# Moving a SwiGLU kernel's stores from GpSimd's queue to ACT's, with the critical section closed without a drain of GpSimd

## The chip, the cores and the metric

The program uses one core of one Trainium2 chip. The metric is device time in microseconds (us), the median of several executions. All executions that are compared here are in the fast state, at a granted clock of 1.0; only e6_hold18, a single look that differs by 14%, has an unknown state. The kernel before takes 938.4 us.

## The reference

```python
def setup_inputs():
    return {"x": np.random.randn(8192, 8192).astype(np.float32)}

def reference(x):
    a, b = np.split(x, 2, axis=-1)
    return a * (b / (1 + np.exp(-b)))        # (8192, 4096)
```

256 MiB are read once and 128 MiB are written once, 402.65 MB in all.

## The kernel before

Two rows of x lie on each partition, so a tile is 128 partitions x 16384 floats (8 MiB), and there are 32 tiles. Three slots hold them in turn. SyncE loads, ACT makes silu of the b half in place, DVE multiplies and packs the product into the front of the same slot, and a store of 4 MiB takes it away. Every engine counts semaphores by hand, inside a critical section in which nothing is ordered automatically. The last tile is cut up so that its last store is small.

```python
def load(i, c0=0, cw=R * M):
    s = i % BUFS
    if i >= BUFS:                                     # the slot must have been stored
        nc.sync.wait_ge(store_sem[s], 16 * (i // BUFS))
    nc.sync.dma_start(out=slots[s][...], in_=xv[...]).then_inc(last_sem if c0 else load_sem[s], 16)

def store(i, eng, c0=0, cw=R * half):
    eng.wait_ge(prod_sem, counts["prod"])             # all products issued so far
    inst = eng.dma_start(out=ov[...], in_=slots[s][:, c0 : c0 + cw])
    # ... completion on store_sem[s], for the last tiles on end_sem

with tc.tile_critical():
    # ... three loads
    for i in range(last):
        swiglu(i)                                     # ACT, then DVE (tile 0 in two halves)
        if i == last - 1:
            swiglu(last, 0, 1)                        # first half of the last tile
        store(i, nc.gpsimd if i < last - 1 else nc.sync)
        # ... load of tile i + 3
    # ... the rest of the last tile; SyncE waits for every store
```

## Time and profile before

| | before |
|---|---|
| median of the first 3 executions | 938.40 us (938.26 to 939.66) |
| profiled span | 936.7 us |
| bytes moved | 402.66 MB, 430 GB/s over the span |
| DMA engines, share of the span | 68.4% loads and the last stores, 31.1% GpSimd's stores |
| DVE / ACT / GpSimd busy | 30% / 24% / 2% |
| last store landed | 933.0 us |
| drain of GpSimd at the end | 2.506 us |

### The profile page before, as it was taken

The numbers are of one execution on the slowest core, as the hardware profiler recorded it, in microseconds if no ns is written. First come the engines' busy times: TensorE is split into PE (matmuls) and PEld (weight loads), VectorE is DVE, ScalarE is ACT, GpSimd is POOL, SyncE is SP. The second block draws the span as 40 slices with busy tenths as digits, with TensorE's granted clock in tenths as the row PEclk, the third lists the DMA queues.
The fourth block names the chain that finished last, engine by engine and source line by source line (L and its number), as shares of the span: only waits on it lengthen the run. The fifth ranks groups of instructions, "written<-read, shape, count | busy, mean of one in ns | idle before, by whom it ended". The sixth has DMA issues, their size and how long they took to land.

```text
span 936.7 us, 196 instructions
## 1 busy us (share of the span) xinstructions
DVE 278.6 (30%) x35; ACT 226.6 (24%) x36; POOL 16.3 (2%) x34
## 2 busy tenths in 40 slices
DVE  0333312333123331233312333213332133331351
ACT  0323331133311333113332033320233302333131
POOL 0000000000000000000000000000000000000000
DMA  9999999999999999999999999999999999999997
GB/s 403 403 448 425 425 448 425 427 441 453 406 465 406 451 423 428 446 424 448 424 448 417 453 413 452 418 439 434 442 425 428 445 424 432 434 453 413 434 435 336
DMA packets 9504, 402.66 MB, mean 430 GB/s; under 512 B 1056, under 2 KB 1056, under 8 KB 1056
## 3 DMA queue, kind: packets, MB, share of 16 engines
q1 hardware_dynamic: 5184, 276.83, 68.4%
q0 software_dynamic: 4320, 125.83, 31.1%
HBM read 268.44 MB, written 134.22 MB: 430 GB/s over the span
## 4 chain that ended last, share of the span: by engine, by line
DMA 80%; DVE 10%; ACT 8%; issue 0%; SPq 0%; DVEq 0%
DMA out_dram<-slot 40%; DMA slot<-in_x_dram 40%; DVE slot L72 10%; ACT slot L67 8%; SPq L48 0%; SPq L138 0%; DVEq L71 0%; SPq L89 0%
## 5 line engine op out<-in xcount | busy, mean ns | idle before, releaser
L72 DVE TENSOR_TENSOR slot<-slot 128x8192 f32<-128x8192 f32 (+2 forms) x35 | 278.6, 7960 | 641.6 <-ACT slot L67 641.5
L67 ACT ACTIVATE slot<-slot 128x8192 f32<-128x8192 f32 (+2 forms) x35 | 225.3, 6443 | 689.8 <-DMA slot<-in_x_dram 689.8
L80 POOL DMA_DIRECT2D out_dram<-slot x30 | 16.1, 536 | 857.8 <-DVE slot L72 857.8
L67 ACT ACT_TABLE_LOAD x1 | 1.3, 1283 | 0.9 <-SPq L89 0.9
L127 POOL MEMSET const-float32-0.0<- 128x1 f32 x1 | 0.1, 98 | 0.2 <-issue 0.2
L127 POOL MEMSET const-bfloat16-1.0<- 128x1 bf16 x1 | 0.1, 101 | 0.0
L127 POOL MEMSET const-float32-1.0<- 128x1 f32 x1 | 0.1, 98 | 0.0
L127 POOL MEMSET const-uint8-127<- 128x1 uint8 x1 | 0.1, 98 | 0.0
## 6 DMA issues: line engine op xcount, KB each, us to landing
out_dram<-slot POOLq DMA_DIRECT2D x30, 4096.0 KB, 37.4
slot<-in_x_dram SPq DMA_DIRECT2D x2, 4096.0 KB, 26.4
out_dram<-slot SPq DMA_DIRECT2D x1, 4096.0 KB, 11.3
out_dram<-slot SPq DMA_DIRECT2D x2, 2048.0 KB, 14.2
slot<-in_x_dram SPq DMA_DIRECT2D x31, 33.6
```

The lines of the kernel that those rows point to most:

```text
L67: nc.scalar.activation(out=b, in_=b, func=_SILU).then_inc(gate_sem, 1)
L72: nc.vector.tensor_mul(out=rows(xt, k0, k1, half, c0, cw), in0=rows(xt, k0, k1, M, c0, cw), in1=b).then_inc(prod_sem, 1)
L80: inst = eng.dma_start(out=ov[i * P : (i + 1) * P, c0 : c0 + cw], in_=slots[s][:, c0 : c0 + cw])
L127: nc = _bacc.Bacc("TRN2", target_bir_lowering=False, num_devices=1)
```

## The change

Its intent: stores off GpSimd's software queue and onto ACT's hardware queue, so that the closing drain of GpSimd can be left out; and one explicit wait less at the end, because the store of tile 29 now counts on the semaphore that the end waits for anyway.

```diff
-        if i < last - 1:
+        if i + BUFS <= last:
             inst.then_inc(store_sem[s], 16)
         else:
             inst.then_inc(end_sem, 16)
             counts["end"] += 1
 
-    with tc.tile_critical():
+    with tc.tile_critical(no_gpsimd_drain=True):
...
-            store(i, nc.gpsimd if i < last - 1 else nc.sync)
+            store(i, nc.scalar if i < last - 1 else nc.sync)
...
-        nc.sync.wait_ge(store_sem[(last - 2) % BUFS], 16 * ((last - 2) // BUFS + 1))
         nc.sync.wait_ge(end_sem, 16 * counts["end"])
```

## The prediction

> **What bounds the kernel now.** I read the page's slices first, then its queues, then the DMA share of chosen windows, then the chain of waits, and last the end of the program, instruction by instruction. The slices and the queues:
>
> ```profile
> DMA  9999999999999999999999999999999999999997
> ...
> q1 hardware_dynamic: 5184, 276.83, 68.4%
> q0 software_dynamic: 4320, 125.83, 31.1%
> HBM read 268.44 MB, written 134.22 MB: 430 GB/s over the span
> ```
>
> The sixteen DMA engines are full in every slice but the last. The two queues together take 68.4 + 31.1 = 99.5% of the span of 936.7 us, so only about 0.5% of it, 4.7 us, has no packet in flight. The remaining 932 us are bytes. Windows cut from the trace (us, busy time of DVE, ACT and POOL, PEclk, DMA share, GB/s) place those 4.7 us:
>
> ```profile
> 0.00:1.50 1.50, 0.00 (x0) 0.59 (x1) 0.20 (x4) 1.00 0.00 0
> ...
> 584.00:671.00 87.00, 26.07 (x3) 21.09 (x3) 1.53 (x4) 1.00 1.00 434
> ...
> 920.00:930.00 10.00, 0.22 (x1) 0.00 (x0) 0.00 (x0) 1.00 1.01 433
> ...
> 933.00:936.70 3.70, 0.00 (x0) 0.00 (x0) 0.00 (x0) 1.00 0.00 0
> ```
>
> About 1 us lies before the first load and 3.7 us after the last store. In the middle, 87 us move three tiles at 434 GB/s with a share of 1.00. The compute engines are far from it: DVE is busy 26 of 87 us.
>
> The chain of waits (start, us, what) walks one slot round and round:
>
> ```profile
> 583.42 0.28 issue
> 583.70 37.41 DMA out_dram<-slot
> 621.11 0.02 issue
> 621.13 33.57 DMA slot<-in_x_dram
> 654.70 0.02 issue
> 654.72 7.04 ACT slot L67
> 661.76 0.02 issue
> 661.78 8.70 DVE slot L72
> ```
>
> One turn of a slot is 37.41 + 33.57 + 7.04 + 8.70 + 0.34 = 87.06 us, and three slots make 29.0 us for each tile. This chain looks like latency, but it isn't: one store carries 4 MiB, which at 434 GB/s takes 9.7 us alone, and one load of 8 MiB takes 19.3 us alone. 9.7 + 19.3 = 29.0 us, exactly the period. The 37 and 34 us are times shared with the other slots' transfers. So shortening one link of this chain lengthens another, as long as the DMA engines have no hole.
>
> The lines that the change does touch at the end are those of the critical section's closing (engine, instruction, count, duration in ns min/median/max, start in us):
>
> ```profile
> L89 SPq NOP  x2: 13/13/13, 0.7 to 935.8; - x2
> ...
> L89 ACTq DRAIN  x1: 8/8/8, 933.3 to 933.3; - x1
> L89 POOLq DRAIN  x1: 2506/2506/2506, 933.3 to 933.3; - x1
> L89 DVEq DRAIN  x1: 10/10/10, 933.3 to 933.3; - x1
> ```
>
> The last store's semaphore arrives at 933.0. Four engines then drain, three of them in about 10 ns; GpSimd takes 2.506 us, and SyncE's closing NOP stands at 935.8 because of it. The list of SyncE's waits has the same: 2.3 us for GpSimd at line 89, once.
>
> **What the Trainium skill says.** "DMA: Bandwidth & Descriptors", section "Issuing engines are not separate DMA queues", says that transfers from the scalar, sync and gpsimd engines all run on the same 16 DMA engines, and that the issuing engine only changes the sequencer time of the start. The trace agrees: the software queue has 125.83 of 402.66 MB, 31.25% of the bytes, for 31.1 of 99.5% of the busy time, 31.26%. A byte costs the same on either queue. The same page, section "Where 436 GB/s comes from", puts the ceiling of the fabric at 435.2 GB/s; the middle of this run measures 434, so I take it for the bound. "SBUF — State Buffer", section "Who interferes with whom", says that a DMA stalled by a DVE operation is a GpSimd-issued one whose descriptors could not be written, but also that tensor_tensor has no two-port mode. This trace shows no such stall: the 30 issues on GpSimd have a minimum and a median of 531 ns, a maximum of 667. On the drain, "VectorE: DVE Perf Modes", section "The DRAIN you can't avoid", knows drains of some 12 ns at the start and end of a program. The trace agrees for ACT, DVE and SyncE (7 to 10 ns) and disagrees by two hundred times for GpSimd here; the measurement decides.
>
> **The change part by part.** I compared the order of instructions of the two builds.
>
> First, the drain. In the changed build GpSimd has no instruction in the critical section any more. It branches straight from the start to the program's final barrier, and the waited-for drain at line 89 is gone; SyncE's closing NOP waits on the drains of ACT, DVE and SyncE alone. GpSimd's own drain before the final barrier has nothing to wait for and runs within the first microseconds, beside the first load. So the NOP moves from 935.8 to about 933.4: 2.4 us saved, all of it on the path that sets the end, because nothing runs beside it. The closing barrier (935.8 to 936.7, 0.9 us) stays; its GpSimd drains were 34, 34 and 96 ns, and one of these leaves the path, 0.1 us. **Sum: -2.5 us.**
>
> Second, the queue. Thirty issues of 531 ns leave GpSimd and thirty come to ACT, where SyncE's three stores cost 333 to 432 ns, say 0.35 us each. 30 x 0.35 = 10 us of ACT, which is busy 226.6 of 936.7 us. Beside that, a store may start some 0.3 to 0.5 us earlier: 0.28 us of issue before GpSimd's instruction against 0.02 to 0.04 us elsewhere in the chain, and 0.53 against 0.35 us of issuing. Times ten turns of the chain this would be 3 to 5 us if the chain were latency. Since the DMA engines are full I count at most what is missing to the ceiling. From the store issue at 60.69 to that at 844.77 there are 27 tiles in 784.08 us, 29.04 us each; 12.58 MB at 435.2 GB/s are 28.91 us. The difference is 0.13 us, times 32 tiles 4 us: that is all there can be to gain, and I expect hardly any. One of the nine turns (321.80 to 409.77) took 87.97 us instead of about 87.0, so 1 us is irregular. I don't know its cause; if it belonged to the software queue it would go. **Sum: 0 to -1 us, I take -0.2.**
>
> Third, the order on ACT. ACT runs in order, so its wait for the product of tile i now stands ahead of the activation of tile i+1. It costs nothing if the product is done before the next load lands. In the chain of starts, DVE ends one tile at 60.39 and the next activation starts at 73.68; later, the store issue at 844.77 stands against the activation at 857.72. The slack is 13 us, against 0.35 us of issuing. The last two stores are SyncE's in both. **Sum: 0.**
>
> Fourth, the counting. The removed wait on SyncE at the end costs one instruction of 17 ns, and the semaphore of tile 29 only moves to the count that is waited for anyway. **Sum: 0.**
>
> In all 938.4 - 2.5 - 0.2 = 935.7 us.
>
> **The rivals.** (a) The latency rival: each store starts 0.5 us earlier and the ten turns give 5 us. The chain of waits speaks for it, the share of 1.00 and the queue shares against it. With the drain gone it would be about 931. (b) The waiting rival: ACT, held by the store's wait, starts activations late, the loads behind them slip and holes open in the DMA row. The 13 us of slack speak against it; were it true for half a microsecond on each tile and not absorbed, 32 x 0.5 = 16 us, about 952. (c) The sharing rival: two hardware queues share the DMA engines differently from one hardware and one software queue, and the rate moves. For it: I have only one long stretch with a software queue in it. Against it: loads alone on the hardware queue ran at 429 GB/s (1 to 23 us), stores alone on it at 433 (920 to 930 us), the mix at 434. One percent either way would be 9 us. (d) The moved drain: the 2.5 us belong to GpSimd's first drain after the start, wherever it stands, and appear again in the final barrier, leaving 938. Against it: GpSimd drains at 0.3 us in the old program already, in 184 ns, and the later drain is before the first tile is finished.
>
> **Range and chances.** The drain's 2.5 us are nearly certain; (d) would take them back. A tail phase that shifts (912 to 920 ran at 389 to 442 GB/s, depending on the cut) is worth plus or minus 1 us. The rest of (a) reaches down to 931, of which I believe half. (c) could pass either limit, with a chance of a few per cent. So 933.0 to 938.0, and within 2% (919.6 to 957.2) nearly certainly: faster 0.02, same 0.96, slower 0.02.
>
> **What would show each step.** Right: no GpSimd drain after 930, and less than 1.5 us from the last store's landing to the span's end instead of 3.7; one kind of queue only, with 402.66 MB at 99.7% or more; the middle windows still 434 GB/s and 29.0 us a tile; ACT's issue groups near 0.35 us, and its activations still ended from idleness by loads, not by DVE. Wrong: a chain whose store links shrink while the load links do not grow (a), ACT waiting for DVE just before late activations (b), a middle rate away from 434 (c), or a 2.5 us drain in the last barrier (d).

## The result, and the profile after

The changed kernel took 936.71 us (median of 6, 935.96 to 937.30), the kernel before in the same rounds 938.44 us (median of 6). The ratio is 0.9978, with a 95% interval from 0.9966 to 0.9991: the mean time of one kernel's fast runs over that of the other's of the same rounds, so not quite the ratio of the two medians. The gain is real and small, 1.7 us.

The slices and the queues of the page after (in the queue lines: packets, MB, share of the 16 engines' span):

```profile
DMA  9999999999999999999999999999999999999998
...
q1 hardware_dynamic: 5184, 276.83, 68.6%
q10 hardware_dynamic: 4320, 125.83, 31.2%
```

The 4320 packets and 125.83 MB that were GpSimd's are now on a second hardware queue. 68.6 + 31.2 = 99.8%, against 99.5% before: there is less idle time at the end, and the same work.

Windows of the trace after (us from and to, length, busy time of DVE, ACT and GpSimd, clock, DMA share, GB/s):

```profile
584.00:671.00 87.00, 26.07 (x4) 21.09 (x3) 0.00 (x0) 1.00 1.00 434
...
934.00:935.00 1.00, 0.00 (x0) 0.00 (x0) 0.00 (x0) 1.00 0.00 0
```

The rate in the middle is the same to the last digit: 434 GB/s at a share of 1.00. From the store issue at 62.56 us to that at 845.57 there are 27 tiles in 783.01 us, 29.00 us each. ACT's activations still wait for loads, and none of them is listed as waiting for DVE (us in total, times, longest us):

```profile
ACT slot L67 <- DMA slot<-in_x_dram: 690.6, 33, 22.1
```

One turn of the chain of waits after (start, us, what):

```profile
584.54 0.02 issue
584.56 36.80 DMA out_dram<-slot
621.36 0.02 issue
621.38 34.38 DMA slot<-in_x_dram
```

The issue ahead of a store fell from 0.28 to 0.02 us and the store's link from 37.41 to 36.80, but the load's link grew from 33.57 to 34.38. What a store got earlier, the load behind it gave back: 36.80 + 34.38 + 7.04 + 8.70 + 0.08 = 87.00 us.

The closing of the critical section after (engine, instruction, count, duration in ns min/median/max, start in us):

```profile
L89 SPq NOP  x2: 13/13/13, 0.7 to 934.2; - x2
...
L89 ACTq DRAIN  x1: 8/8/8, 934.0 to 934.0; - x1
L89 DVEq DRAIN  x1: 10/10/10, 934.0 to 934.0; - x1
```

GpSimd's drain is gone and the NOP follows the other drains at once. But they start at 934.0, where they started at 933.3 before. By the records of the semaphores, the last store landed at 933.80 us, where it landed at 932.98 before. So the two spans divide like this:

```
                         before      after     difference
last store landed        932.98     933.80        +0.82
from there to the end      3.68       1.24        -2.44
span                     936.66     935.04        -1.62
```

The end gained what was predicted. In front of it, 0.8 us were lost. The experiments ask what makes GpSimd's drain long, which part of the change removes it, whether the start of a store matters, and where the 0.8 us come from.

Where they come from can already be narrowed. These are the first activations of tile 1 in the timelines of the two kernels, before and then after (start, us, engine, line, operation):

```profile
44.63 7.03 ACT L67 ACTIVATE slot<-slot 128x8192 f32<-128x8192 f32 x1 [14.54 <-DMA slot<-in_x_dram]
```

```profile
46.77 7.03 ACT L67 ACTIVATE slot<-slot 128x8192 f32<-128x8192 f32 x1 [16.61 <-DMA slot<-in_x_dram]
```

The load of tile 1 landed 2.1 us later; the first store (issued at 35.6 us) had started while this load was under way. A transfer adds to its semaphore sixteen times. Before, the sixteen increments of this load came within 0.69 us (43.91 to 44.60); after, fourteen came from 44.61 to 45.39 and the last two at 46.73 and 46.75. Most of the transfer had not become much slower; two parts of sixteen had. I strung the packet records of each trace end to end into sixteen sequences, one for each DMA engine (the records don't name the engine, so this is a reconstruction). A packet of 64 KiB takes 2.418 us nearly always. When the first store enters, at about 39 us, all sixteen sequences of the kernel before and fourteen of the kernel after show one slow packet of 3.2 to 3.9 us. The other two of the kernel after have two slow ones in place of it, of 3.2 to 3.3 us at 37 us and of 4.0 to 4.2 us at 41 us, some 2.4 to 2.5 us over the usual length in place of 0.8 to 1.5. In the reconstruction they lie about 1 us behind from there on and never catch up, since they have work all the time. At the end most of the other engines stand idle near 912.8 us for 0.2 to 1.4 us, while the late ones still bring the last piece of the last load, which ACT, DVE and the last store wait for.

### The profile page after: what moved, and what is told of

Its sections match the earlier page's. It is cut to its first block, busy times and chain, and to the rows that moved or that the text cites. A ratio compares the mean times of both kernels' runs of the same rounds, so it can differ in the third digit from the quotient of the medians.

```text
span 935.0 us, 192 instructions
## 1 busy us (share of the span) xinstructions
DVE 278.6 (30%) x35; ACT 226.6 (24%) x36; POOL 0.2 (0%) x4
## 3 DMA queue, kind: packets, MB, share of 16 engines
q1 hardware_dynamic: 5184, 276.83, 68.6%
q10 hardware_dynamic: 4320, 125.83, 31.2%
## 4 chain that ended last, share of the span: by engine, by line
DMA 81%; DVE 10%; ACT 8%; issue 0%; SPq 0%; DVEq 0%
DMA slot<-in_x_dram 41%; DMA out_dram<-slot 39%; DVE slot L72 10%; ACT slot L67 8%; SPq L48 0%; SPq L137 0%; DVEq L71 0%; SPq L89 0%
```

## The experiments

Twelve runs were made, two of them of the changed kernel itself; all gave correct results. A time that is compared with the changed kernel's 936.7 us comes from other rounds, unless it is said otherwise. The line numbers in their profiles shift a little with their edits.

### e0_after and e13_after_again: the changed kernel again

No edit.

> The changed kernel again, only for more executions and a second trace. It ended 0.8 us later than the drain alone accounts for, because one DMA engine of sixteen lagged from the second load on. If that lag is an accident of each execution, the times scatter between about 936.0 (no lag: the full 2.4 us of the drain) and 937.3, and this trace may show the last store landing near 933.0. If it belongs to the ACT queue, every execution is near 936.7 and the second load again lands about 2 us later than in the kernel before.

> The changed kernel as it is, in the same rounds as the kernel with the first store held back: near 936.7 (935.96 to 937.3 so far), second load landing near 46.7 us.

The first took 936.72 us (5 executions, 936.05 to 937.07), the second 936.86 (5, 936.41 to 937.42). With the first six, sixteen executions lie between 935.96 and 937.42. The trace of the first shows the lag again: fourteen increments of tile 1's load from 44.05 to 44.57 and two at 46.61 and 46.69, the last store landed at 933.70. In the trace of the second, an execution of 936.41 us, tile 1's activation starts where it did in the kernel before:

```profile
44.91 7.03 ACT L67 ACTIVATE slot<-slot 128x8192 f32<-128x8192 f32 x1 [14.98 <-DMA slot<-in_x_dram]
```

The spread is 43.93 to 44.89, and the last store landed at 933.39. In the packet records of this trace no sequence is slow twice. So the early lag is not in every execution of the same program; two of its three traces have it. It is not the whole of the 0.8 us either: without it the last store still landed 0.41 us later than in the kernel before.

### e1_pool_nodrain: the flag alone

```diff
-    with tc.tile_critical():
+    with tc.tile_critical(no_gpsimd_drain=True):
```

(on the kernel before; stores stay on GpSimd)

> The kernel before with the flag for no GpSimd drain alone; stores stay on GpSimd. Drain theory: 938.4 - 2.4 = 936.0, span 934.3, last landing still 933.0. If the ACT queue itself costs the 0.8 us that were missing, this one is faster than the changed kernel by about 0.7 us. Rival (moved drain): GpSimd has issued DMAs, so the 2.5 us appear in the final barrier and the time stays 938.4.

It took 938.36 us against 938.40, ratio 1.0001 (0.9989 to 1.0014): nothing gained. The drain was not saved. This is GpSimd's group of drains in the program's final barrier (count, ns min/median/max, start of first and last):

```profile
L138 POOLq DRAIN  x3: 34/96/2506, 933.1 to 936.1; - x3
```

One of the three took 2506 ns, to the nanosecond what it took before in the section's closing, and it started at 933.1. In the built program, GpSimd's drain at the closing is replaced by an instruction that does nothing but wait for SyncE's end of the section. The trace has it as a NOP after the last store has landed (932.75 us), and behind it stands the barrier's drain:

```profile
L89 POOLq NOP  x1: 13/13/13, 933.0 to 933.0; - x1
```

The "moved drain" rival, which the prediction argued against, is what happens as long as the stores stay on GpSimd.

The opposite half needs no run. The changed kernel built without the flag is, instruction for instruction, the same program as with it (the two builds were compared, neither was run for this): GpSimd has no instruction in the section, so it is not drained there in any case. The whole effect at the end comes from the move of the stores. The flag alone gave nothing, and beside the move it changes nothing.

### e3_act_memset, e4_act_one_pool, e9_half_pool: what makes the drain long

All three are the changed kernel with the default closing, in which GpSimd's drain stands in the path if GpSimd has any instruction in the section. They give GpSimd a memset, one store, and fifteen stores.

```diff
# e3_act_memset
+        nc.gpsimd.memset(spare[:, :], 0.0)
# e4_act_one_pool (that store's completion on a semaphore of its own)
-            store(i, nc.scalar if i < last - 1 else nc.sync)
+            store(i, nc.gpsimd if i == 0 else nc.scalar if i < last - 1 else nc.sync)
# e9_half_pool (likewise)
+            store(i, nc.gpsimd if i < 15 else nc.scalar if i < last - 1 else nc.sync)
```

> The changed kernel with the default closing and one tiny GpSimd memset at the start of the critical section, so that GpSimd is in the section and its drain stands at the end, but it has issued no DMA. If the 2.5 us belong to any GpSimd drain in that place: the time of the changed kernel + 2.4, 939.1. If they belong to a drain after GpSimd has issued DMAs: the drain is under 0.2 us and the time is that of the changed kernel, about 936.7.

> The changed kernel with the default closing and only the first of the thirty stores on GpSimd, its completion counted on a semaphore of its own. If a drain is dear because GpSimd has issued a DMA at all: a drain of 2.5 us at the end although the one DMA landed 860 us earlier, time about 939.1. If the cost grows with the number of DMAs issued: 2.5 / 30 = 0.1 us more than the changed kernel, 936.8.

> The changed kernel with the default closing and the first fifteen of the thirty stores on GpSimd, the other fifteen on ACT. GpSimd's drain took 2506 ns after 30 of its DMAs, 130 ns after 1 and 41 ns after none. If it costs some 82 ns for each DMA issued: 41 + 15 x 82 = 1.27 us at the end. If it is long only when GpSimd has issued DMAs late in the run (the last one at 874 us in the kernel before): here GpSimd is quiet for the second half, and the drain is 0.1 us.

GpSimd's drain at the closing of e3_act_memset, of e4_act_one_pool and of e9_half_pool:

```profile
L90 POOLq DRAIN  x1: 41/41/41, 934.0 to 934.0; - x1
```

```profile
L95 POOLq DRAIN  x1: 130/130/130, 933.4 to 933.4; - x1
```

```profile
L96 POOLq DRAIN  x1: 1281/1281/1281, 933.2 to 933.2; - x1
```

With the 2506 ns of the kernel before, there are four points: 0, 1, 15 and 30 DMAs on GpSimd, 41, 130, 1281 and 2506 ns. The first DMA adds 89 ns, the next fourteen (1281 - 130) / 14 = 82 ns each, the last fifteen (2506 - 1281) / 15 = 82 ns each. So the drain at the closing costs 41 ns and some 82 ns for each of GpSimd's stores. (That an earlier drain of GpSimd resets the count is shown by e10_pool_drained below.) All of these stores have the same shape, 4 MiB in 144 packets, so the runs don't tell whether the cost grows with the DMAs, their packets or their bytes. In e9_half_pool the last of them was issued near the middle of the run (438.9 us), and in e4_act_one_pool at its start, and each still costs 82 to 89 ns, so waiting long after the last DMA doesn't remove the cost. The expectation of 1.27 us was met to 0.01 us.

The times: e3 936.82 us (936.15 to 936.94), e4 936.25 (936.04 to 936.28), e9 937.53 (937.16 to 937.91). The longer drain, 1.15 us more in e9 than in e4, accounts for nearly all of the 1.28 us between the two medians, which come from different rounds and chips. e4 has no early lag (increments of tile 1's load from 43.94 to 44.86) and is the only kernel with stores on ACT whose five executions all lie below 936.3.

### e10_pool_drained: the backlog cleared out of sight

```diff
             store(i, nc.gpsimd if i < last - 1 else nc.sync)
+            if i == last - 2:
+                nc.gpsimd.drain()
```

(on the kernel before; default closing)

> The kernel before, stores on GpSimd and the default closing, with one more drain of GpSimd put in right after its last store is issued (874 us), where GpSimd has 59 us of nothing to do. If the drain's cost is a backlog of the thirty DMAs that the first drain clears: that drain takes some 2.4 us out of sight, the closing one 0.05 to 0.2 us, and the time is 938.4 - 2.4 = 936.0. If every drain after GpSimd's DMAs costs 2.5 us: the closing one still does and the time is 938.4.

It took 936.07 us (5 executions, 935.92 to 936.48) against 938.37, ratio 0.9976 (0.9963 to 0.9990). The added drain and the closing one:

```profile
L102 POOLq DRAIN  x1: 31132/31132/31132, 872.6 to 872.6; - x1
```

```profile
L89 POOLq DRAIN  x1: 41/41/41, 933.0 to 933.0; - x1
```

The added one takes 31.1 us, far over the 2.4 expected: the last GpSimd store, issued at 872.6, landed at 902.4, and the drain ended at 872.6 + 31.1 = 903.7, 1.3 us after that. This fits a drain that also waits for GpSimd's own DMAs; one trace can't show more. Nobody waits for GpSimd then, so this costs nothing, and the closing drain finds nothing left: 41 ns, as if GpSimd had issued no DMA. The price is a backlog, not a property of every drain on GpSimd.

This kernel keeps its stores on GpSimd and its median lies 0.6 us below that of the changed kernel, which was measured in other rounds. That is the best of the twelve; the interval of its ratio overlaps that of the changed kernel (0.9966 to 0.9991), so I don't call it faster than that one.

### e5_hold2 and e6_hold18: does the start of a store matter, and the order on ACT

```diff
         eng.wait_ge(prod_sem, counts["prod"])
+        if i < last - 1:
+            for _ in range(1):          # 9 in e6_hold18
+                nc.scalar.activation(out=spare[:, :], in_=spare[:, :], func=_SILU).then_inc(hold_sem, 1)
+                counts["hold"] += 1
+                nc.scalar.wait_ge(hold_sem, counts["hold"])
```

> The changed kernel, with about 2 us of activation on a spare tile held between the wait for the product and each of ACT's thirty stores. If the time of a store's start sets the run (latency theory, ten turns of the chain): 936.7 + 10 x 2 = 957. If the DMA engines set it and only the sum of bytes counts: within 1 us of the changed kernel, 936 to 938, with the load or store links of the chain shorter by the 2 us that were put in.

> The same with nine such activations before each store, about 17 to 18 us. ACT then has 7.0 (activation) + 8.7 (wait for DVE) + 17.5 + 0.4 = 33.6 us for each tile, more than the 29.0 that the DMA engines need. If ACT's order of program is what holds the next activation behind the store (the waiting rival, past its 13 us of slack): about 30 x 33.6 + 65 = 1070 us, with ACT no longer released by loads but by itself. If the slack is larger than I read it: still 937.

e5_hold2 took 937.25 us (937.22 to 937.65). Thirty stores start 1.9 us later each, and the time is 0.5 us more than that of the changed kernel, not 20. Its middle window and its chain:

```profile
584.00:671.00 87.00, 26.08 (x4) 26.82 (x6) 0.00 (x0) 1.00 1.00 434
```

```profile
239.34 34.95 DMA out_dram<-slot
274.30 34.29 DMA slot<-in_x_dram
```

The rate is 434 GB/s still, and the store's link is 1.85 us shorter than in the changed kernel (34.95 against 36.80), which is what was put in ahead of it. The latency rival is refuted by the time, 0.5 us more and not 20: the links of the chain stretch to fill the time that the DMA engines need for the bytes.

e6_hold18 took 1074.2 us (one look), 1070 were expected. Here ACT is the bound. Its waits:

```profile
ACT spare L84 <- DVE slot L74: 259.4, 30, 8.8
ACT L69 <- DMA slot<-in_x_dram: 22.9, 1, 22.9
ACT slot L69 <- ACT spare L84: 12.5, 30, 0.5
```

Except for the first load, ACT never waits for a load; it stands up to 8.8 us, thirty times, for DVE, ahead of a store, with the next activation behind it. So the waiting rival is a real mechanism. A hold of 1.9 us left ACT waiting for loads, one of 17.4 us did not; the 13 us of slack that the prediction read lie between the two, but the edge itself was not measured. The changed kernel uses 0.34 us of it.

### e8_early: the hole at the end filled

```diff
+            store(i, nc.scalar if i < last - 1 else nc.sync)
             if i == last - 1:
                 swiglu(last, 0, 1)
-            store(i, nc.scalar if i < last - 1 else nc.sync)
```

> The changed kernel with the store of tile 30 placed before the first half of tile 31, so that it waits for its own product alone (some 903.5 us) and not for that of the half tile (912.8 us). In the changed kernel's trace most DMA engines stand idle for about 1 us near 912.8 because that store isn't there yet while one lagging engine still brings the last load. On the same queue the store comes behind the load on each engine. If that hole is what the lag costs: 1.0 us less than the changed kernel, 935.7, and less scatter, because engines that are done with the load go on with the store. If the last load is delayed by the store as much as the hole is worth: 936.7.

It took 936.97 us (936.82 to 937.20), near the second branch of the expectation (936.7); the first, 935.7, failed. The hole is filled: none of the sixteen reconstructed sequences has a gap over 0.15 us near 912.8 any more, and thirteen end at 932.0 to 932.5 us. But three lagged in this trace, and the last of them ends at 933.77, and the last store landed at 934.16. So idle time of the engines that are ahead was not the cost: the engines that lagged ended last with the hole on the others or without it. From the last increment of the last load to the landing of the last store it is 19.36 us here, with the hole filled, and 19.40 us in the changed kernel, with the hole.

### e7_warm and e12_hold_first: why the lag

```diff
# e7_warm, first in the section
+        nc.scalar.dma_start(out=spare[:, :], in_=xv[:P, :1024]).then_inc(warm_sem, 16)
# e12_hold_first: the hold of e5_hold2, for the first store alone, on 512 columns
+        if i == 0:
```

> The changed kernel with one small load (512 KB, unused) issued on ACT at the very start, so that ACT's queue has been used before its first store. If one DMA engine is held up twice because the ACT queue is used for the first time in mid-stream: no such lag at the second load, times near 936.0 + 1.2 us for the 0.5 MB more that are moved at 434 GB/s, and little scatter. If the lag comes with the first store whatever was before it: the lag stays and the time is near 936.7 + 1.2 = 937.9.

> The changed kernel with the very first store alone held back by some 0.6 to 0.7 us (one small activation on a spare tile), so that it starts when the kernel before started it (35.8 + 0.5 us of issuing on GpSimd, against 35.6 on ACT). If the one lagging DMA engine is only a matter of the moment at which the first store meets the stream of load packets: no lag, the second load's last engine lands near 44.8 us instead of 46.7, times near 936.1. If it belongs to the first store coming over ACT's queue: the second load still lands near 46.7 us and the times are near 936.7.

e7_warm took 937.56 us (937.40 to 937.86), between the two expectations of 937.2 and 937.9. The increments of tile 1's load still spread from 45.32 to 47.29: nine came by 45.94, seven from 46.96 on. In the packet records, nine packets are slow near 40 us, and seven near 42 us with smaller delays near 38 us before them. A queue that had been used before did not prevent the lag.

e12_hold_first took 937.53 us (937.52 to 938.02), more than the changed kernel in the same rounds (936.86), where 936.1 or 936.7 was expected. It is not a clean test: the added wait also moved ACT's table load from 0.9 to 23.0 us, so that the first store was issued 1.9 us later than in the changed kernel, not 0.65. And slow packets came at 41 us (two of sixteen already at 39) and again at 75 to 82 us, around the second store; the trace of e5_hold2, whose table load had moved in the same way, has them there too. This start, 1.9 us later, was no cure. Both runs are inconclusive as to the cause.

What the traces do show is how the lag sets the end. In all thirteen in which the DMA engines are the bound (e6_hold18 is left out), the last store lands 19.35 to 19.55 us after the last increment of the last load. For the nine traces in which that load's first increment comes at the same time, these are the increments of its last piece, first and last of sixteen, and the landing of the last store (us):

```
trace               first store on   last load landed      spread   last store landed
e10_pool_drained    GpSimd           912.85 to 913.36       0.51        932.76
e9_half_pool        GpSimd           912.98 to 913.54       0.56        932.94
e1_pool_nodrain     GpSimd           912.65 to 913.33       0.68        932.75
before              GpSimd           912.77 to 913.57       0.80        932.98
e4_act_one_pool     GpSimd           912.85 to 913.75       0.90        933.16
e13_after_again     ACT              912.82 to 913.84       1.02        933.39
e0_after            ACT              912.89 to 914.33       1.44        933.70
e3_act_memset       ACT              912.92 to 914.45       1.53        933.82
after               ACT              912.83 to 914.40       1.57        933.80
```

The engine that comes first is there at 912.65 to 912.98 in all of them, so between these nine the spread decides, and the last store's landing follows it almost one to one. (In e5_hold2, e7_warm and e12_hold_first even the first increment comes at 914.02 to 914.27, and in e8_early the order of the tail differs.) The five traces whose first store came from GpSimd have spreads of 0.51 to 0.90, the four whose first store came from ACT 1.02 to 1.57. The runs on chip 3 alone divide in the same way: 0.68 and 0.90 against 1.44 and 1.53. In the packet records around the first store, no sequence is slow twice in any of the five traces with that store on GpSimd; one to three are in e3_act_memset, e0_after, after and e8_early, none in e13_after_again. That the first store's queue has a part in it is likely from this, though every kernel but the changed one has one trace only. Why some engines are held up twice there stays open.

A caution on reading spreads: only the last one is a loss. In the middle of a run a spread of 1.8 to 2.8 us, about one packet of 2.42 us, also occurs where little is lost. In the trace before, the increments of one store come within 0.6 us up to 360 us and are 2.6 us apart from 389 us on, and still the last load has a spread of 0.80. I read this as one engine taking its packets in another order; no run tests that.

## Why the prediction was right or wrong

It was right: 935.7 us with a range of 933.0 to 938.0, and 936.71 measured. Of the gain of 2.7 us that it foresaw, 1.7 came. That the total came so near rests on the drain, whose place on the path was read rightly; the queue's term had the wrong sign. Step by step:

- **The drain, -2.5 us: right.** The part of the span after the last landing went from 3.68 to 1.24 us, -2.44. The reading was right that GpSimd leaves the section because it has no instruction in it. The prediction gave no reason for the 2.5 us, and the runs give one: 82 ns for each of thirty stores on GpSimd. It did not say that the flag thus has nothing left to do; the comparison of the builds and e1_pool_nodrain show that.
- **The queue, -0.2 us (0 to -1): the term that was mis-sized.** It measured +0.82 in the pair of traces, the later landing of the last store; against the other two traces of the changed kernel it is +0.72 and +0.41. (The 4 us that the prediction set as the most to gain there are an estimate from the 435.2 GB/s of the page that it names.) The prediction asked whether a byte costs the same on both queues, and it does: the mean rate of the middle stayed at 434 GB/s with both. It did not look at the sixteen increments of each load one by one, and so did not see that one or two engines out of sixteen can decide. An average share of 1.00 says nothing about that.
- **The earlier start of stores: right that it is worth hardly anything.** It came (0.28 to 0.02 us of issue in the chain, 531 to 339 ns for the issuing instruction) and was given back in the load's link; e5_hold2 shows the same from the other side.
- **The order on ACT, 0: right.** ACT's activations are still released by loads, and e6_hold18 shows what it takes to break that.
- **The rivals.** The latency rival and the waiting rival were rightly set aside. The sharing rival did not show in the rate. The moved-drain rival was set aside for two reasons, of which one is poor: the drain of 184 ns at the start stands before GpSimd has issued any DMA, so it had no backlog. The other, that GpSimd's later drain comes before the first tile is finished, holds in the changed kernel (0.7 us), whose GpSimd has no backlog at all; e1_pool_nodrain shows that the rival holds for the flag alone.
- **The irregular turn of 1 us before.** It falls where the spread of one store's increments jumps from 0.6 to 2.6 us. In e10_pool_drained, with the same queues, no spread exceeds 0.8 us. So it does not belong to the software queue as such. Its absence takes 1.07 us off the 27 tiles after (783.01 against 784.08), but that is no gain at the end: e10_pool_drained, which lacks it too, has its last store only 0.22 us earlier than the kernel before.
- **A reading that was off.** The prediction puts about 1 us before the first load; by the packet records, the first packet starts at 1.95 us. Both kernels have it, so no sum changes.

## What to carry to other kernels

Here the DMA engines were full from end to end, and moving transfers to another queue bought nothing in the middle; in such a kernel, look at what stands before the first byte and after the last. In these runs a drain of GpSimd cleared a backlog that grew with the stores it had issued: keep them off GpSimd where the drain ends the program, or drain GpSimd early where nobody waits for it, and check in the trace that a flag has removed the wait and not only moved it. When a transfer that ends a chain is late, compare the first with the last of its sixteen increments before blaming the rate.

## What the Trainium skill lacked or had wrong

- "VectorE: DVE Perf Modes", section "The DRAIN you can't avoid", gives some 12 ns for the drains around a program, on all five engines. ACT, DVE and SyncE agree with 7 to 10 ns. GpSimd does not: 184 ns at the start of the program before, and, at the closing of the critical section, 41 ns without DMAs of its own and 2506 ns after thirty. (The section speaks of the runtime's drains and has nothing on one that the program itself places, as this one.)
- "DMA: Bandwidth & Descriptors", section "SWDGE vs HWDGE vs iDMA", names a faster setup as the advantage of the hardware queues. It lacks what a DMA on GpSimd's software queue costs later: some 82 ns for each 4 MiB store at GpSimd's next drain, and that a drain right behind such a DMA lasts until after it has landed (31.1 us in e10_pool_drained).
- No page that I read tells that single DMA engines of the sixteen can lose about 1 us more than the others at the moment when a second queue's first transfer enters, and that the end of the run then follows the last of them (spreads of 0.51 to 1.57 us, last store at 932.76 to 933.82 us). Why it happens is open here too.
